# Two transformer blocks in one kernel: the down products on six PSUM banks, other queues, buffers and layout for the state space tables

## The chip, the cores and the metric

The kernel runs on one core of a Trainium2 chip. A core has TensorE (PE; its weight loads are listed apart as PEld), VectorE (DVE), ScalarE (ACT), GpSimd (POOL) and SyncE (SP), and 16 DMA engines that copy between the chip's memory and the on-chip memory. PE writes its results to PSUM, a small memory in banks, from which DVE and ACT read them; everything else lies in SBUF. SP and POOL each have a queue of their own from which they issue DMAs, and an instruction in a queue waits behind the one ahead of it.

The metric is the time of one execution on the device, in microseconds, as the median of several runs.

## The reference

One sequence of 1024 tokens with 1024 features goes through two blocks, in float32.

```python
x = layer_norm(ALPHA * x + 0.5 * swiglu(x, ffn1_w1, ffn1_w3, ffn1_w2), ln1_g, ln1_b)
q_lat, kv_lat, k_rope, u, g_a, g_b = split(x @ w_in)       # 384, 256, 32, 512, 1024, 1024 columns
y_a = mla_attention(q_lat, kv_lat, k_rope, ...) @ w_o_attn   # 8 heads; the latents are RMS-normed first
y_b = s5_branch(u, ...) @ w_o_ssm                            # 32 groups of 16 channels, 64 complex states
merged = sigmoid(g_a) * y_a + sigmoid(g_b) * y_b
x = layer_norm(ALPHA * x + merged @ w_out, ln2_g, ln2_b)
x = layer_norm(ALPHA * x + 0.5 * swiglu(x, ffn2_w1, ffn2_w3, ffn2_w2), ln3_g, ln3_b)
ple = sigmoid(x @ ple_w_gate) * (p @ ple_w_proj)
x = layer_norm(ALPHA * x + ple, ln4_g, ln4_b)
return second_block(x, ...)                                  # RG-LRU, convolutions, pooling, one gated mixer
```

`swiglu(x, w1, w3, w2) = (silu(x @ w1) * (x @ w3)) @ w2`, with 2816 hidden features. The S5 branch is a linear recurrence over the tokens in both directions. The kernel computes it in blocks of eight tokens, with tables made from the parameters: powers of the discretised state matrix times the input and output matrices B and C.

## The kernel before

Every matrix product is done in three passes: each float32 operand is split into a rounded high part and a remainder, and PE multiplies high by low, low by high and high by high. A split is a cast on ACT (L80) and a subtraction on DVE (L81). Weights pass through the ring `raw` (three buffers of 128 x 1024 words), loaded by SP; their parts are `wh` and `wl`.

PSUM has three rings: `up` (two tiles of two banks), `dn` (two tiles of one bank) and `tr` (two tiles of one bank). `tr` is for transposes above all, of the tables (L689, L709, L729, L730) as of the normalised rows (L144), and for the sums of squares (L955).

**The down projection** (`ffn_down`, called for both feed-forwards) computes the product of the hidden features `h` and the weights `V` by seven products of half size instead of eight. Product `i` has 11 steps of 12 matmuls (four row tiles `t`, three passes), 132 matmuls of 512 columns (L390). Products 0, 2, 4 and 6 write four half tiles of the two `up` tiles (`even`); products 1, 3 and 5 write two `dn` and two `tr` tiles (`odd`). After each product its four tiles are copied or added to `acc`, eight tiles of 128 x 1024 (ACT after products 0 and 1, DVE behind the others). Products 0 to 3 split the hidden features, which come back from memory, on the way; later ones load the parts. `half(0)`, after product 5, normalises the first four row tiles and transposes them into `x`, the input of the next projection; `half(1)` does so for the others after product 6. `affine` (L1269, L1270) then finishes the rows, and they are stored to `xd`.

**The tables** are made by a generator that hands over between two pieces of work. In the first feed-forward, `tick` runs it two steps at a time after each sixth of a product: `s5_setup`, then `s5_tables` for the batches 0 to 2 of eight, in the memory called `arena`. Per batch: POOL loads B and C (L684, L685), PE transposes C, DVE multiplies complex numbers in many small instructions (L470 to L477 and L654 to L658), PE transposes the results (L709, L729, L730), and POOL stores seven tables to `sd`. A second arena, opened after the first feed-forward in the memory that `acc` had, goes on with batches 3 to 7 beside the next projections; what it keeps of the first one comes by way of the memory `kd`.

**The gates** come after the latents: 16 blocks of 48 matmuls, each followed by a tanh into the ring `g` (two buffers) and a store to `gd` by SP (L933). Between them stand the five sums of squares of the latents (`squares`, L952 and L955, which use the same ring `g`) and, from the fifth block on, the state space batches: `s5_load` brings the tables (`s5b_tab`, L757, on SP) and the inputs (`s5b_U`, L760, eight loads on POOL), two batches ahead, and `s5_batch` begins with L782.

The order on each engine is made when the kernel is built, by a scheduler that simulates the engines with costs of its own. Program order decides which buffer of a ring a tile gets, and an instruction waits for whoever had that buffer before.

Of the kernel before, what the change touches and what calls it, by code (L numbers as in the profile page):

```python
# [8 lines left out]
F32 = mybir.dt.float32  # L9
# [8 lines left out]
P = 128  # L18
S = 1024
# [10 lines left out]
class Net:  # L30
# [314 lines left out]
    def ffn_down(self, fp, vr, acc, w2, hd, scale, load, half, tick=lambda: None):  # L345


        nc, v = self.nc, self.nc.vector
        hf, hs = hd
        NP = NF // 2  # L350
        units = [(i, min(2, NP - i)) for i in range(0, NP, 2)]
        wv = w2.rearrange("(q j p) m -> j p q m", j=2, p=P)
        rp = vr.enter_context(self.pool("vr", side="right"))

        first = [rp.tile([P, n, HALF], F32, name=self.uid("V")) for n in (8, NP - 8)]
        V = {k: rp.tile([P, NP, HALF], F32, name=self.uid("V")) for k in ((1, 1), (0, 1))}

        def at(k, ps):
            if k != (0, 0):
                return V[k][:, ps]  # L360
            return first[0][:, ps] if ps.stop <= 8 else first[1][:, ps.start - 8:ps.stop - 8]

        def loads(k):
            for p0, n in units:
                nc.sync.dma_start(at(k, slice(p0, p0 + n)), wv[k[0], :, p0:p0 + n, k[1] * HALF:(k[1] + 1) * HALF])

        def plus(x, y, op=ALU.add):
            v.tensor_tensor(out=x, in0=x, in1=y, op=op)

        def product(i, k, out, add=None, also=None):  # L370

            for u, (p0, n) in enumerate(units):
                ps = slice(p0, p0 + n)
                if add:
                    plus(at(k, ps), at(add, ps))
                if also:
                    also(ps)
                z = fp.tile([P, 2, 2, HALF], F32R, tag="v", bufs=2, name=self.uid("v"))
                self.split(at(k, ps), hi=z[:, 0, :n], lo=z[:, 1, :n])
                if i < 4:  # L380
                    h = self.split(self.raw(hf[i, :, ps], [P, n, HALF]))
                else:
                    h = [self.stream.tile([P, n, HALF], F32R, tag=tg, bufs=3, name=self.uid("h")) for tg in ("wh", "wl")]
                    for e in range(2):
                        nc.sync.dma_start(h[e].bitcast(F32), hs[i - 4, :, u, e, :n])
                for kk in range(n):
                    for t in range(4):
                        tk = slice(t * P, (t + 1) * P)
                        for m, (a, b) in enumerate(((0, 1), (1, 0), (0, 0))):
                            nc.tensor.matmul(out[t], lhsT=h[a][:, kk, tk], rhs=z[:, b, kk],  # L390
                                             start=u + kk + m == 0, stop=p0 + kk == NP - 1 and m == 2)
                tick()

        def even():
            ps = [self.up() for _ in range(2)]
            return [ps[j // 2][:, (j % 2) * HALF:(j % 2 + 1) * HALF] for j in range(4)]

        def odd():
            return [self.dn(), self.dn(), self.tr(), self.tr()]
        lo, hi = slice(0, HALF), slice(HALF, D)  # L400

        def residual(h):
            for t in range(h * 4, h * 4 + 4):
                x = self.stream.tile([P, D], F32, tag="raw", bufs=3, name=self.uid("res"))
                load(t, x)
                v.scalar_tensor_tensor(out=acc[t], in0=x, scalar=scale, in1=acc[t], op0=ALU.mult, op1=ALU.add)

        p = even()
        loads((0, 0))
        product(0, (0, 0), p)  # L410
        V[1, 0] = fp.tile([P, NP, HALF], F32, name=self.uid("V"))
        loads((0, 1))
        for t in range(4):
            nc.scalar.copy(acc[t][:, lo], p[t])
            nc.scalar.copy(acc[4 + t][:, lo], p[t])
        p = odd()
        product(1, (0, 0), p, add=(0, 1))
        loads((1, 0))
        for t in range(4):
            nc.scalar.copy(acc[t][:, hi], p[t])  # L420
            nc.scalar.copy(acc[4 + t][:, hi], p[t])
        p = even()
        product(2, (1, 0), p)
        loads((1, 1))
        for t in range(4):
            plus(acc[t][:, lo], p[t])
        p = odd()
        product(3, (1, 1), p)
        for t in range(4):
            plus(acc[t][:, hi], p[t])  # L430
        residual(0)
        p = even()
        product(4, (0, 0), p, add=(1, 1))
        for t in range(4):
            plus(acc[4 + t][:, lo], p[t])
            plus(acc[t][:, hi], acc[4 + t][:, lo], ALU.subtract)
        p = odd()
        product(5, (0, 1), p, add=(1, 1), also=lambda ps: plus(V[1, 0][:, ps], at((0, 0), ps)))
        for t in range(4):
            plus(acc[4 + t][:, lo], p[t])  # L440
            plus(acc[4 + t][:, hi], acc[4 + t][:, lo], ALU.subtract)
        vr.close()
        half(0)
        residual(1)
        p = even()
        product(6, (1, 0), p)
        for t in range(4):
            plus(acc[4 + t][:, lo], p[t])
        half(1)
# [6 lines left out]
GB = 4  # L456
# [3 lines left out]
class S5(Net):  # L460
# [96 lines left out]
    def s5_setup(self, arena):  # L557
# [14 lines left out]
        v.memset(at(2176, [P, G]), 0.0)  # L572
        nc.gpsimd.dma_start(dT, I["ssm_d"][0].rearrange("g c -> c g"))
        yield "pe"
        pt = self.tr()
        for i in range(2):
            nc.tensor.transpose(pt[:, i * G:(i + 1) * G], rows[:, i, :], self.ident[:G, :G])
# [83 lines left out]
    def s5_tables(self, arena, pool, sd, batches):  # L661
# [13 lines left out]
        vk = lambda z: z.rearrange("p (g a b) -> p g a b", g=GB, a=8)  # L675
        for i in range(2):
            v.memset(bd[i], 0.0)
        for b in batches:
            gs = slice(b * GB, (b + 1) * GB)
            R = [at(3840 + N * (i + 3 * (b % sets)), [P, N]) for i in range(3)]  # L680
            s4 = [pool.tile([P, N], F32, tag="tf", bufs=2, name=self.uid("s4")) for _ in range(2)]
            for d, s in enumerate("fb"):
                for i, nm in enumerate(("re", "im")):
                    nc.gpsimd.dma_start(B[d * 64:(d + 1) * 64, i], I[f"ssm_b_{nm}_{s}"][0, gs].rearrange("g p c -> p g c"))  # L684
                    nc.gpsimd.dma_start(crow[:, i, d * 64:(d + 1) * 64], I[f"ssm_c_{nm}_{s}"][0, gs].rearrange("g c p -> (g c) p"))  # L685
            yield "pe"
            pt = self.tr()
            for i in range(2):
# [3 lines left out]
            pair = lambda z: [z[:, 0], z[:, 1]]  # L692
            self.cmul(pair(bb), bc(be), pair(B), s2)
            self.cmul(pair(Br), bc(f), pair(bb), s2)
            yield

            def powers(tab, coef, o):
# [56 lines left out]

    def s5_load(self, b, pool, sd, ud):
        tab = pool.tile([P, 7, GB * NCH], F32, tag="s5b_tab", bufs=2, name=self.uid("s5b_tab"))
        self.nc.sync.dma_start(tab, sd[b])  # L757
        U = pool.tile([P, GB, NCH], F32, tag="s5b_U", bufs=2, name=self.uid("s5b_U"))
        for t in range(T8):
            self.nc.gpsimd.dma_start(U[t * C16:(t + 1) * C16],  # L760
                                   ud[b * GB * C16:(b + 1) * GB * C16, t, :].rearrange("(g c) k -> c g k", c=C16))
        return tab, U
# [67 lines left out]
class Mid(S5):  # L830
# [68 lines left out]
    def latents(self, xT, apool, gpool):  # L899
# [13 lines left out]
        for o, z in zip(wide, n0):  # L913
            z = z.bitcast(F32)
            nc.vector.tensor_copy(o[:, :, 0:96].rearrange("p k (a m) -> p k a m", a=3),
                                  z.unsqueeze(2).to_broadcast([P, KD, 3, 32]))
            nc.vector.tensor_copy(o[:, :, 96:112], z[:, :, 16:32])
            nc.vector.tensor_copy(o[:, :, 112:128], z[:, :, 0:16])
        p = self.up()
        for h in range(2):  # L920
            self.mm3(p[:, h * HALF:(h + 1) * HALF], [((wide[0][:, k], wide[1][:, k]), (xh(k, h), xl(k, h))) for k in range(KD)])
# [22 lines left out]
    def rms_latents(self, lat, tmp):  # L944
# [3 lines left out]
        sc = self.small.tile([P, 5, 8], F32, tag="rmss", bufs=1, name="rmss")  # L948

        def squares(k, tmp):  # L950
            t = tmp.tile([P, S], F32, tag="g", bufs=2, name=self.uid("sq"))
            nc.scalar.activation(out=t, in_=lat[k], func=AF.Square)  # L952
            ss = self.tr()
            for tt in range(8):
                nc.tensor.matmul(ss[:, tt:tt + 1], lhsT=t[:, tt * P:(tt + 1) * P], rhs=self.ones[:, 0:1], start=True, stop=True)  # L955
            v.tensor_copy(sc[:, k], ss[:, :8])
# [204 lines left out]
class Mix(Mid):  # L1161
# [133 lines left out]
    def block1(self):  # L1295
# [55 lines left out]
        xa.close()  # L1351
        q0.close()
        with self.pool("ffn1") as fp:
            acc = [fp.tile([P, D], F32, name=self.uid("acc")) for _ in range(8)]
            for nm in ("tf", "tf"):
                fp.tile([P, HALF], F32, tag=nm, bufs=2, name=self.uid("tf"))
            arena = fp.tile([P, 5376], F32, name="arena")
            kd = self.dram.tile([P, self.KEEP], F32, name="kd")

# [14 lines left out]
            def load(t, x):  # L1374
                nc.sync.dma_start(x, I["x"][0, t * P:(t + 1) * P, :])
# [20 lines left out]

        ap = LS.enter_context(self.pool("A"))
        self.rt = ap.tile([P, S], F32, name="rt")
        nc.sync.dma_start(self.rt[64:128], I["k_rope"])
        tabs = ExitStack()  # L1400
        tp = tabs.enter_context(self.pool("tabs"))
        arena = tp.tile([P, 6912], F32, name="arena")
# [863 lines left out]
```

## Time and profile before

| | us |
|---|---|
| median of 3 runs | 3318.21 (3316.32 to 3318.26) |
| profiled run | 3317.19 |
| its span in the profile | 3315.4 |
| PE busy | 3096.7 (93%) |
| DVE busy | 2455.5 (74%) |
| ACT busy | 1311.4 (40%) |
| POOL busy | 203.4 (6%) |

The shares are averages over stages with different limits. PE's mean granted clock over the span is 0.968 of full speed. A matmul that comes first after an idle stretch can run at the lower clock, so an idle stretch on PE costs more than its own length. In the page's strip of 40 slices PE has its lowest digits in slices 1, 6, 8, 9 and 10, and 12 and 13, that is in the first 80 us, from 480 to 520, from 600 to 840 and from 1000 to 1060 us.

### The profile page before, as it was taken

To read this page: it belongs to the slowest core of one execution; us is meant where nothing else is said; L and a number is where in the kernel's file an instruction comes from. 1 tells how busy PE (TensorE), PEld (TensorE's weight loads), DVE (VectorE), ACT (ScalarE), POOL (GpSimd) and SP (SyncE) were. 2 spreads that over 40 slices of the span, in tenths; PEclk is the share of its full clock that TensorE was granted. 3 is DMA by queue.
4 is the path that set the end of the run, shared out by engine and by line. 5 is a ranking of instruction groups with operands and counts; after the bars stand their busy time and mean duration, and the time that the engine had idled before them with its cause. 6 is when DMAs were issued, how large, how long until landed. Compare 5 with 4: busy or idle time off the path is not lost. (4 is left out here: it accounts for less than half of the span.)

```text
span 3315.4 us, 38710 instructions
## 1 busy us (share of the span) xinstructions
PE 3096.7 (93%) x14237; PEld 2516.1 (76%) x14237; DVE 2455.5 (74%) x4082; ACT 1311.4 (40%) x1857; POOL 203.4 (6%) x407
## 2 busy tenths in 40 slices
PE   6999988688996999999998999979989999999998
PEld 5788867566785878887876887868878788888786
DVE  6887767867565667776588886756778498898668
ACT  4233323223221136663263333333244456555443
POOL 0000000211343320000000000000000000000000
PEclk8999999898997999999998999989999999999999
DMA  3543445354534520004454544363733222322545
GB/s 121 160 151 121 134 162 182 107 201 137 161 111 142 172 82 9 17 7 159 165 169 137 165 146 124 130 250 105 245 116 109 89 70 82 97 85 72 193 159 182
DMA packets 334011, 433.17 MB, mean 131 GB/s; under 512 B 29861, under 2 KB 218302, under 8 KB 332542
## 3 DMA queue, kind: packets, MB, share of 16 engines
q1 hardware_dynamic: 319486, 408.45, 37.6%
q0 software_dynamic: 14336, 22.26, 2.2%
q8 instruction: 112, 1.84, 0.2%
q14 instruction: 77, 0.63, 0.1%
HBM read 311.00 MB, written 119.62 MB: 130 GB/s over the span
## 5 line engine op out<-in xcount | busy, mean ns | idle before, releaser
L101 PE MATMUL up<-x,wh 128*128 128x512 f32 x2336 | 755.8, 400 | 15.2 <-DVE x L81 13.9
L101 PEld LDWEIGHTS up<-x,wh 128*128 128x128 f32 x2336 | 442.5, 190 | 125.8 <-DVE x L81 16.9
L80 ACT CAST wh<-raw 128x1024 fp32r<-128x1024 f32 (+2 forms) x305 | 307.6, 1011 | 426.9 <-PE up L176 179.3
L101 PE MATMUL up<-x,wl 128*128 128x512 f32 x1168 | 465.5, 399 | 0.3 <-DVE wl L81 0.3
L81 DVE TENSOR_TENSOR wl<-raw,wh 128x1024 fp32r<-128x1024 f32 (+2 forms) x305 | 356.6, 1170 | 144.1 <-ACT wh L80 143.4
L1260 PE MATMUL up<-wh,x 128*128 128x512 f32 x1024 | 319.4, 393 | 0.0
L101 PEld LDWEIGHTS up<-x,wl 128*128 128x128 f32 x1168 | 221.9, 190 | 52.4 <-DVE wl L81 0.8
L1260 PEld LDWEIGHTS up<-wh,x 128*128 128x128 f32 x1024 | 192.2, 188 | 41.9 <-DVE x L81 0.8
L1260 PE MATMUL up<-wl,x 128*128 128x512 f32 x512 | 201.9, 396 | 2.5 <-ACT xf L2157 1.8
L80 ACT CAST v<-V 128x1024 fp32r<-128x1024 f32 x84 | 82.2, 981 | 271.4 <-PE up L390 127.5
L81 DVE TENSOR_TENSOR v<-V,v 128x1024 fp32r<-128x1024 f32 x84 | 94.9, 1131 | 93.2 <-ACT v L80 93.1
L390 PE MATMUL up<-v,wh 128*128 128x512 f32 x352 | 117.5, 412 | 41.1 <-DVE v L81 41.0
L80 ACT CAST wh<-S 128x1024 fp32r<-128x1024 f32 x88 | 73.3, 833 | 204.4 <-PE dn L176 141.8
L2078 DVE SCALAR_TENSOR_TENSOR cv<-u,kc,cv 128x1024 f32<-128x1024 f32 x120 | 153.0, 1275 | 1.2
L390 PE MATMUL up<-v,h 128*128 128x512 f32 x528 | 126.1, 394 | 0.7 <-DVE v L81 0.7
L1260 PEld LDWEIGHTS up<-wl,x 128*128 128x128 f32 x512 | 96.1, 188 | 26.3 <-ACT xf L2157 2.4
L390 PEld LDWEIGHTS up<-v,wh 128*128 128x128 f32 x352 | 70.3, 200 | 59.1 <-DVE v L81 43.7
L390 PEld LDWEIGHTS up<-v,h 128*128 128x128 f32 x528 | 97.5, 188 | 22.6 <-DVE v L81 2.7
L176 PE MATMUL up<-x4l,wh 128*128 128x512 f32 x176 | 73.3, 416 | 42.9 <-ACT wh L80 41.4
L101 PE MATMUL up<-k,qh 128*128 128x512 f32 x256 | 93.1, 406 | 2.3 <-ACT e L1087 2.3
L80 ACT CAST ph<-tr 128x512 fp32r<-128x512 f32 x128 | 73.6, 587 | 51.7 <-PE tr L1100 50.7
L81 DVE TENSOR_TENSOR pl<-tr,ph 128x512 fp32r<-128x512 f32 x128 | 85.6, 682 | 10.6 <-ACT ph L80 10.1
(651 smaller groups left out, 7058.8 us busy)
## 6 DMA issues: line engine op xcount, KB each, us to landing
raw<-in_ffn_w_dram SPq DMA_DIRECT2D x96, 512.0 KB
raw<-in_w_in_dram SPq DMA_DIRECT2D x69, 512.0 KB
hs<-sp SPq DMA_DIRECT2D x66, 512.0 KB
h<-hs SPq DMA_DIRECT2D x60, 512.0 KB
raw<-in_w_out_dram SPq DMA_DIRECT2D x52, 512.0 KB
raw<-hf SPq DMA_DIRECT2D x40, 512.0 KB
V<-in_ffn_w_dram SPq DMA_DIRECT2D x40, 512.0 KB
s5b_tab<-sd SPq DMA_DIRECT2D x8, 1792.0 KB
```

The costliest lines, as they stand in the source:

```text
L80: (copy or nc.scalar.copy)(hi, x)
L81: nc.vector.tensor_tensor(out=lo, in0=x, in1=hi.bitcast(F32), op=ALU.subtract)
L101: nc.tensor.matmul(out, lhsT=a, rhs=b, start=i == 0, stop=i == n - 1)
L176: nc.tensor.matmul(out, lhsT=w[a][:, k], rhs=x[b][:, kx], start=start and i == 0, stop=stop and i == 11)
L390: nc.tensor.matmul(out[t], lhsT=h[a][:, kk, tk], rhs=z[:, b, kk], start=u + kk + m == 0, stop=p0 + kk == NP - 1 and m == 2)
L1260: self.nc.tensor.matmul(o, lhsT=a, rhs=b[:, c], start=k == 0 and m == 0, stop=k == K - 1 and m == 2)
L2078: v.scalar_tensor_tensor(out=st["y"], in0=u[:, j:j + S], scalar=k, in1=st["y"], op0=ALU.mult, op1=ALU.add)
```

## The change

There are five edits.

1. `odd` takes two `dn` tiles and one `up` tile (its two halves for row tiles 2 and 3) instead of two `dn` and two `tr`. The list `late` empties the `up` halves first. Where a result goes to two places in `acc`, the second is now made from the first in SBUF, in a loop of its own.
2. `s5_setup` yields once more before its first transpose. `s5_tables` loads B and C for the next batch right after their last use in this one.
3. `s5_load` issues the load of the tables from POOL instead of SP.
4. In the pool of the first feed-forward the two `tf` tiles come first, then `acc` in reverse, so that other tiles lie where the second arena is opened. The load of `rt` (the rope table) is issued later, among the latents.
5. `squares` takes its buffer from the ring `raw` instead of `g`.

```diff
         def odd():
-            return [self.dn(), self.dn(), self.tr(), self.tr()]
+            ps = [self.dn(), self.dn(), self.up()]
+            return ps[:2] + [ps[2][:, :HALF], ps[2][:, HALF:]]
+        late = (2, 3, 0, 1)
...
         for t in range(4):
             nc.scalar.copy(acc[t][:, lo], p[t])
-            nc.scalar.copy(acc[4 + t][:, lo], p[t])
+        for t in range(4):
+            nc.scalar.copy(acc[4 + t][:, lo], acc[t][:, lo])
...
         p = odd()
         product(3, (1, 1), p)
-        for t in range(4):
+        for t in late:
             plus(acc[t][:, hi], p[t])
...
+        yield "pe"
         yield "pe"
         pt = self.tr()
...
+        def load(b):
+            gs = slice(b * GB, (b + 1) * GB)
+            for d, s in enumerate("fb"):
+                for i, nm in enumerate(("re", "im")):
+                    nc.gpsimd.dma_start(B[d * 64:(d + 1) * 64, i], I[f"ssm_b_{nm}_{s}"][0, gs].rearrange("g p c -> p g c"))
+                    nc.gpsimd.dma_start(crow[:, i, d * 64:(d + 1) * 64], I[f"ssm_c_{nm}_{s}"][0, gs].rearrange("g c p -> (g c) p"))
+        load(batches[0])
         for b in batches:
...
             self.cmul(pair(Br), bc(f), pair(bb), s2)
+            if b != batches[-1]:
+                load(b + 1)
             yield
...
-        self.nc.sync.dma_start(tab, sd[b])
+        self.nc.gpsimd.dma_start(tab, sd[b])
...
+        nc.sync.dma_start(self.rt[64:128], self.I["k_rope"])
         p = self.up()
...
-            t = tmp.tile([P, S], F32, tag="g", bufs=2, name=self.uid("sq"))
+            t = self.stream.tile([P, S], F32, tag="raw", bufs=3, name=self.uid("sq"))
...
-            acc = [fp.tile([P, D], F32, name=self.uid("acc")) for _ in range(8)]
             for nm in ("tf", "tf"):
                 fp.tile([P, HALF], F32, tag=nm, bufs=2, name=self.uid("tf"))
+            acc = [fp.tile([P, D], F32, name=self.uid("acc")) for _ in range(8)][::-1]
...
-        nc.sync.dma_start(self.rt[64:128], I["k_rope"])
```

The edits also move instructions on the engines, since the scheduler orders anew. Line numbers after the change are 13 to 14 higher from `s5_tables` on: the table transposes L689, L709, L729 and L730 are L700, L722, L742 and L743 there, the squares' matmuls L955 are L969, and L782 is L795. Three places matter.

On PE, in product 3 of the first down projection (its tiles are `dn_4618`, `dn_4619`, `tr_4620`, `tr_4621`), before:

```order
2300 L390 MATMUL dn_4619<-v_4658,wl_4664 128x512
2301 L390 MATMUL dn_4619<-v_4658,wh_4663 128x512
2302 L689 MATMUL tr_4235<-ident,arena 128x64 x2
2303 L709 MATMUL tr_4313<-ident,arena 128x128 x4
2304 L709 MATMUL tr_4320<-ident,arena 128x128 x4
2305 L729 MATMUL tr_4455<-arena 64x128
2306 L689 MATMUL tr_4589<-ident,arena 128x64 x2
2307 L390 MATMUL tr_4620<-v_4622,wh_4627 128x512
2308 L390 MATMUL tr_4620<-v_4622,wl_4628 128x512
```

and the same product now (its tiles are `dn_4598`, `dn_4599` and `up_4600`):

```order
2272 L390 MATMUL dn_4599<-v_4601,wh_4606 128x512
2273 L390 MATMUL dn_4599<-v_4601,wl_4607 128x512
2274 L390 MATMUL dn_4599<-v_4601,wh_4606 128x512
2275 L390 MATMUL up_4600<-v_4601,wh_4606 128x512
2276 L390 MATMUL up_4600<-v_4601,wl_4607 128x512
```

Before, two units of the product on the `dn` tiles are followed by the transposes of two table batches, and the `tr` tiles come after them. Now the four tiles of a step follow each other, and the first table transpose (L700) stands at row 2392, at the end of the product.

On DVE, at the same product, before (`arena` holds the tables; the split ahead of these rows, of `v_4658`, is row 781, and the next one, of `v_4705`, row 902):

```order
786 L470 TENSOR_TENSOR arena<-arena 128x256
787 L471 TENSOR_TENSOR arena<-arena 128x256
788 L472 TENSOR_TENSOR arena<-arena 128x256
789 L470 TENSOR_TENSOR arena<-arena 128x32
790 L471 TENSOR_TENSOR arena<-arena 128x32
791 L472 TENSOR_TENSOR arena<-arena 128x32
792 L475 TENSOR_TENSOR arena<-arena 128x256
```

and now, where L470 to L477 are L476 to L483, and `V` and `raw` are what is split:

```order
797 L481 TENSOR_TENSOR arena<-arena 128x256
798 L81 TENSOR_TENSOR v_4744<-V_3615,v_4744 128x1024
799 L481 TENSOR_TENSOR arena<-arena 128x32
800 L482 TENSOR_TENSOR arena<-arena 128x256
801 L661 TENSOR_TENSOR arena<-arena 128x512
802 L81 TENSOR_TENSOR wl_4789<-raw_4786,wh_4788 128x1024
803 L482 TENSOR_TENSOR arena<-arena 128x32
```

The rows before are part of 120 table instructions in a row. Now a split stands after 31 of them at most, here after two to four.

On PE, in the gate stage, where the last tables are transposed and the first state space batch begins, before:

```order
3629 L729 MATMUL tr_7100<-arena 64x128
3630 L730 MATMUL tr_7100<-arena 64x128
3631 L955 MATMUL tr_7212<-ones,sq_7210 128x1 x8
3632 L955 MATMUL tr_7282<-ones,sq_7280 128x1 x8
3633 L782 MATMUL up_7305<-s5b_U_7143,s5b_tab_7141 128x128 x8
3634 L816 MATMUL dn_7344<-s5b_U_7143,s5b_tab_7141 128x128
3635 L101 MATMUL up_7373<-x_5380,wh_7369 128x512
```

and now:

```order
3588 L101 MATMUL up_7225<-x_5378,wl_7222 128x512
3589 L101 MATMUL up_7225<-x_5378,wh_7221 128x512
3590 L969 MATMUL tr_7279<-ones,sq_7277 128x1 x8
3591 L743 MATMUL tr_7097<-arena 64x128
3592 L742 MATMUL tr_7097<-arena 64x128
```

The sums of squares stood between the last transpose and the first batch; the second of them now stands in row 3590, the first in row 3585, ahead of the last transposes; the first batch (L795) follows these directly, in row 3598. On POOL the table load of a batch stands directly ahead of its eight U loads for batches 0 and 1, and behind them for the others.

## Rows read from the trace of the kernel before

**Rows 1.** The page, busy time, share of the span and instructions of each engine.

```profile
PE 3096.7 (93%) x14237; PEld 2516.1 (76%) x14237; DVE 2455.5 (74%) x4082; ACT 1311.4 (40%) x1857; POOL 203.4 (6%) x407
```

**Rows 2.** Windows: length, busy us of PE, PEld, DVE, ACT, POOL; clock, DMA share, GB/s.

```profile
600.60:784.60 184.00, 146.09 (x638) 116.07 (x638) 133.39 (x292) 46.69 (x59) 44.46 (x84) 0.89 0.50 169
700.00:740.00 40.00, 29.61 (x110) 23.06 (x109) 23.01 (x58) 10.42 (x11) 3.28 (x7) 0.83 0.40 145
784.60:836.00 51.40, 35.33 (x128) 26.14 (x129) 37.10 (x70) 14.93 (x20) 0.00 (x0) 0.78 0.27 96
860.00:1000.00 140.00, 140.00 (x668) 111.47 (x667) 82.58 (x173) 33.73 (x46) 56.53 (x107) 1.00 0.38 115
1000.00:1046.00 46.00, 18.16 (x84) 15.85 (x83) 11.22 (x30) 7.92 (x10) 18.61 (x37) 0.66 0.51 170
1020.00:1040.00 20.00, 3.03 (x15) 2.94 (x14) 0.39 (x5) 1.46 (x2) 11.53 (x23) 0.50 0.80 272
1046.00:1190.00 144.00, 143.83 (x756) 121.81 (x756) 101.63 (x173) 25.45 (x31) 48.54 (x96) 0.99 0.52 155
2220.00:2420.00 200.00, 199.25 (x893) 163.20 (x891) 144.02 (x181) 74.94 (x92) 0.00 (x0) 1.00 0.52 173
```

**Rows 3.** Timeline of PE, 597 to 647: start, us, instruction, count, [idle before, releaser].

```profile
597.81 0.39 PE L390 MATMUL up<-v,wl 128*128 128x512 f32 x1
...
600.08 0.39 PE L390 MATMUL up<-v,wh 128*128 128x512 f32 x1
...
620.48 0.46 PE L689 MATMUL tr<-ident,arena 64*128 64x64 f32 x2 [11.84 <-DMA arena<-in_ssm_c_re_f_dram]
...
646.66 0.80 PE L390 MATMUL dn<-v,wh 128*128 128x512 f32 x1 [3.87 <-DVE v L81]
```

**Rows 4.** Timeline of DVE, two splits of V that follow each other.

```profile
604.32 1.22 DVE L81 TENSOR_TENSOR v<-V,v 128x1024 fp32r<-128x1024 f32 x1
...
645.40 1.21 DVE L81 TENSOR_TENSOR v<-V,v 128x1024 fp32r<-128x1024 f32 x1
```

**Rows 5.** Waits of PE, 660 to 780: us in total, times, longest.

```profile
PE dn L390 <- DVE v L81: 7.0, 2, 5.3
PE tr L709 <- DVE nq L109: 2.3, 1, 2.3
PE tr L709 <- DVE nq L113: 1.1, 1, 1.1
```

**Rows 6.** The first window of rows 2, matmuls of L390 alone (PE, PEld).

```profile
600.60:784.60 184.00, 132.13 (x528) 102.87 (x528) 0.89 0.50 169
```

**Rows 7.** Groups of DVE, 600.6 to 784.6: count, busy us, mean ns, idle before.

```profile
L368 DVE TENSOR_TENSOR acc<-acc,up 128x512 f32<-128x512 f32 x8 | 5.0, 678 | 0.0
L81 DVE TENSOR_TENSOR x<-tf,x 128x512 fp32r<-128x512 f32 x7 | 4.6, 686 | 2.2 <-ACT x L80 2.2
L150 DVE TENSOR_SCALAR tf<-tr,vecs 128x512 f32<-128x512 f32 x4 | 3.2, 802 | 0.4 <-PE tr L144 0.4
```

**Rows 8.** Timeline of PE in the gate stage.

```profile
1041.13 3.57 PE L955 MATMUL tr<-ones,sq 128*128 128x1 f32 x16 [18.10 <-ACT sq L952]
1044.57 3.76 PE L782 MATMUL up<-s5b_U,s5b_tab 128*128 128x128 f32 x16
```

**Rows 9.** Timelines of SP's queue and of ACT, same stage.

```profile
1024.64 0.81 SPq L757 DMA_DIRECT2D s5b_tab<-sd  x2
...
1040.02 1.06 ACT L952 ACTIVATE sq<-lat 128x1024 f32<-128x1024 f32 x1 [15.87 <-DMA gd<-g]
```

**Rows 10.** DMA issues, 1000 to 1300: count, KB each, median us to landing.

```profile
s5b_tab<-sd SPq DMA_DIRECT2D x8, 1792.0 KB
...
s5b_U<-ud POOLq DMA_DIRECT2D x64, 32.0 KB, 7.2
```

**Rows 11.** Timeline of POOL, the U loads of two batches.

```profile
1064.22 4.04 POOL L760 DMA_DIRECT2D s5b_U<-ud  x8 [26.14 <-PE dn L817]
...
1109.53 4.04 POOL L760 DMA_DIRECT2D s5b_U<-ud  x8 [17.58 <-PE dn L817]
```

More of the change, by code (lines that the diff above doesn't have):

```diff
@@ L418, in ffn_down @@
         loads((1, 0))
-        for t in range(4):
+        for t in late:
             nc.scalar.copy(acc[t][:, hi], p[t])
-            nc.scalar.copy(acc[4 + t][:, hi], p[t])
+        for t in late:
+            nc.scalar.copy(acc[4 + t][:, hi], acc[t][:, hi])
         p = even()
@@ L428, in ffn_down @@
         product(3, (1, 1), p)
-        for t in range(4):
+        for t in late:
             plus(acc[t][:, hi], p[t])
@@ L435, in ffn_down @@
             plus(acc[4 + t][:, lo], p[t])
+        for t in range(4):
             plus(acc[t][:, hi], acc[4 + t][:, lo], ALU.subtract)
@@ L438, in ffn_down @@
         product(5, (0, 1), p, add=(1, 1), also=lambda ps: plus(V[1, 0][:, ps], at((0, 0), ps)))
-        for t in range(4):
+        for t in late:
             plus(acc[4 + t][:, lo], p[t])
+        for t in late:
             plus(acc[4 + t][:, hi], acc[4 + t][:, lo], ALU.subtract)
@@ L681, in s5_tables @@
             s4 = [pool.tile([P, N], F32, tag="tf", bufs=2, name=self.uid("s4")) for _ in range(2)]
[L682 to L685, printed above, removed]
             yield "pe"
```

## The prediction

> **What bounds the kernel now.** I read the page first, then PE by stretches of time, then its timeline and waits where it is idle. The page [rows 1] shows PE busy for 3096.7 us of a span of 3315.4: an edit is worth what it takes out of the 219 us of idle, and of the stretches beside them at the lower clock. The profiled run took 3317.19 us, so 1.8 us lie around the span; the median of the three runs shown, 3318.21, is 1.0 us above that run. I sum against the profiled run and add the 1.0 at the end.
>
> The stretches [rows 2] show where the idle time stands in the part that the change touches. Products 3 to 6 of the first down projection (600.6 to 784.6 us) last 184.0 us with PE busy 146.1 and a mean granted clock of 0.89. The tail behind them (to 836) lasts 51.4 with PE busy 35.3. In the gate stage, 1000 to 1046, PE works 18.2 of 46. The down projection of the second feed-forward, which has no tables beside it, is busy 199.25 of 200 us: the product loop as such has nothing to give.
>
> Inside products 3 to 6 the first stall is the large one. PE's timeline [rows 3] shows it standing 11.84 us for a table transpose (L689) at 620.48, which waits for the load of its operand; it comes back to the `dn` columns of product 3 only at 646.66. Product 3's last two columns could not be written meanwhile, because both `tr` banks belonged to the tables. DVE meanwhile ran tables: between the split of V at 604.32 and the next at 645.40 there is none [rows 4]. Later in the same products PE waits 7.0 + 2.3 + 1.1 us for DVE, while DVE normalises half 0 [rows 5].
>
> **Part 1: six PSUM banks, table loads a batch ahead, the extra stop in the setup.** These have one answer. Product 3 now writes `dn`, `dn` and one `up` tile, so no table transpose stands in front of its columns: the first moves from PE row 2302 to row 2392, the end of product 3. The B and C loads are issued right after the previous batch's last use of their buffers, so L689's 11.84 us go, unless DVE is late. On DVE the block of 120 table instructions between two splits of V becomes at most 31.
>
> What bounds the stretch then? PE's floor: ten matmul starts lie between 597.81 and 600.08 [rows 3], 0.227 us each; 4 products x 132 x 0.227 = 119.9 us. All other PE work in the stretch is 146.1 - 132.1 = 14.0 us [rows 2, 6], together 134. DVE's floor: 133.4 us busy [rows 2], less the seven L81 x splits and four L150 of half 0 (4.6 + 3.2 = 7.8 us) [rows 7], which now stand behind product 6: 125.6. The two are close, so I don't take the floor of PE. The 10.4 us of waits on half 0's norm [rows 5] have not lost their cause; I keep them, and 3.4 us for the lower clock beside them (a granted 0.83 over the 40 us from 700 leaves 6.8 us short, and half of that is PE's own). 134 + 14 = 148 us against 184: **-36**. The bounds are 134 (PE never waits: -50) and 168 (the tables keep half of what they took: -16). I take 148, nearer to 134, because the row without tables shows the loop itself running without a break.
>
> **The tail.** Half 0's 32 feature transposes (L144) stood inside product 6; they now come after it, since the two `tr` banks they rotate through are held by table tiles that trail. So 7.8 us of DVE work move from beside product 6 to the tail, on top of 37.1 us there [rows 2]: 44.9 at least, 51.4 + 7.8 = 59.2 at most. PE has only 24 of the next matmuls to put between them. I take 55.4, near the upper end, because the x splits stand in one queue with sixteen affine operations there: **+4** (-6.5 to +7.8).
>
> **The new bank ring.** An odd product's `up` tile takes the slot of the even product before it. Its first `up` column comes after six `dn` matmuls, 1.4 us; emptying two half tiles is two additions of 0.68 us [rows 7], queued behind at most one split of 1.2 [rows 4]. So a change of product costs 0 to 2 us, and there are six in each projection; the second one is fully busy now, so nothing there hides a wait. I take **+1** in each, bounds 0 and +6. The evacuation copies that now read SBUF stay on ACT, which is busy 47 of the 184 us: nothing, and about 0.5 us per change if ACT were late.
>
> **Part 2: the squares and the table load (gates).** PE stands 18.10 us before the squares' matmuls L955 at 1041.13 [rows 8]: ACT's square waited 15.87 us for the `gd<-g` store to free the ring, and that store stood on SP behind the two L757 loads, which left at 1024.64 when the table stores had landed [rows 9]. With the square in the weight ring both squares' matmuls stand before L730 and wait for no store. Next is L782, and now its operands are late: from 1024.64 POOL issues the table (1792 KB, 6.6 us at the 272 GB/s of 1020 to 1040 in rows 2) and then eight U loads (4.0 us of issue, 7.2 to land) [rows 10, 11]. U is the last: 1024.6 + 0.5 + 4.0 + 7.2 = 1036.3. L782 started at 1044.57, so **-8**; the 7 us of square matmuls move into the idle time and are in the 8. Were U there as soon as it is issued, it would be -15; with both tables ahead of it on the wires (13.2 us) and U behind, -1. A new wait comes along: a weight load needs a ring slot that PE must first read at L955, and the rest of SP's queue stands behind it. The next gate's 48 matmuls (11 us) cover one load; uncovered it would be 512 KB at the 170 GB/s of 1000 to 1046, 3 us for each of five squares.
>
> **Part 3: layout and the rope load.** The second arena now lies under columns that finish earlier. But PE is busy without a break from 860 to 1000 with DVE at 83 of 140 us [rows 2], so an earlier start is hidden: 0, down to -4 if the last table ended earlier too. The rope load waits for nothing where it now stands: 0.
>
> Sum: -36 + 4 + 1 + 1 - 8 = -38; 3317.2 - 38 + 1.0 = **3280 us**.
>
> **A rule against the table load's move.** The eight U loads of a batch leave POOL in 4.04 us [rows 11], 0.505 each, in a stretch where DVE is busy 101.6 of 144 us [rows 2]. The Trainium skill (SBUF — State Buffer, "Who interferes with whom") says that a DMA issued by GpSimd can be held up by DVE, because GpSimd writes the descriptors through a port pair that it shares with DVE, and that issuing it from a hardware queue ends this. The trace's even 0.505 us does not show it; by the rule the load had better stayed on SP, and the third rival is what it would do here.
>
> **Rivals.**
> 1. The stall only moves. DVE's floor is 125.6 of 148 us, and half 0 now ends later: the stretch takes 168 us (-16), the tail 59 (+8), the ring +2, the gates -4. That is -10: 3308. For it: all of PE's later waits [rows 5] are for DVE, and DVE and PE have nearly the same floor. Against: no block of more than 31 table instructions is left.
> 2. Both stalls go with their low clock: 134 us (-50), tail 45 (-6), gates -15, arena -4, ring 0: -75, 3243. Against: the waits of [rows 5] keep their cause.
> 3. Slower: POOL's queue becomes the bound of the eight state space batches. In a pair of batches (1064.22 to 1109.53) POOL idles 17.6 us [rows 11]. Two table loads in that queue bring 2 x (0.5 + 6.6) = 14.2 if something behind waits for their landing, so 3.4 are left. Were POOL's 32 issues of 0.5 us in a pair also twice as long beside DVE, +16, each pair would be 13 over; three pairs cost 39 us and the gates' gain is gone: -36 + 4 + 2 + 39 = +9, 3327. The kernel gets slower from 10 us over per pair. Against: the loads are issued two batches ahead.
> 4. It doesn't do what it says: tables still come between, since they trail and now hold `tr` ahead of half 0's features; the stretch gains 6, the tail gives it back, the gates gain 1: 3317.
>
> **Chances.** The forecast 0.62, with a range of its own from 3262 to 3299 (the stretch -50 to -18, tail and gates within their bounds, not all at one end). Rival 1 0.15; rival 2 0.08; rival 3 0.07; rival 4 0.08. For 8 times in 10 the range runs from 3252, half way to rival 2, to 3311, which takes in rival 1. About 0.2%, 6.6 us, can be told from no change. Faster is the forecast with rivals 1 and 2: 0.85; same is rival 4: 0.08; slower is rival 3: 0.07.
>
> **What would show it.** Right: no gap of 11.84 us in product 3; PE idle under 18 us from product 3 to the end of product 6, which ends 30 us or more earlier; in the gates no wait for the square, and in its place one of 10 to 15 us before L782, on a DMA. Wrong: PE's waits for the V splits in products 3 to 6 as long in sum as before (rival 1); PE waiting for U or the table in each batch after 1046 (rival 3); in the second projection waits of `up` for the additions at every change of product, above 2 us each.

## The result, and the profile after

The changed kernel takes **3258.01 us** (median of four runs, 3256.48 to 3260.63), against 3318.24 of the kernel before in the same measurement; the ratio is 0.982, 95% interval 0.9808 to 0.9832. That is 60 us less where 38 were forecast. The direction held, and so did the range for 8 times in 10, 3252 to 3311; the forecast's own, 3262 to 3299, was missed by 4 us. The profiled run took 3256.48 us, with a span of 3254.7.

The page's first line shows the same work with less idle time on PE, 174 us of the span instead of 219 [rows 1]:

```profile
PE 3080.6 (95%) x14237; PEld 2507.4 (77%) x14237; DVE 2457.0 (75%) x4082; ACT 1312.7 (40%) x1857; POOL 207.9 (6%) x415
```

The windows that answer to rows 2 are products 3 to 6, the tail behind them, and the gate stage up to the first state space batch (length, busy us of PE, PEld, DVE, ACT and POOL, then clock, DMA share, GB/s):

```profile
598.00:732.50 134.50, 129.68 (x592) 104.59 (x590) 121.61 (x283) 39.21 (x47) 35.25 (x66) 1.00 0.66 220
732.50:784.00 51.50, 34.24 (x147) 25.72 (x147) 43.31 (x85) 21.53 (x32) 14.46 (x27) 0.75 0.32 112
955.00:995.00 40.00, 14.94 (x84) 12.62 (x83) 12.28 (x37) 5.81 (x8) 17.32 (x34) 0.64 0.58 178
980.00:995.00 15.00, 0.16 (x1) 0.19 (x2) 0.00 (x0) 0.00 (x0) 7.56 (x16) 0.50 0.63 194
```

Products 3 to 6 last 134.5 us instead of 184.0, at a granted clock of 1.00. DVE did not bound them: it is busy 121.6 us. All waits of PE in them are these three groups (us in total, times, longest), 4.8 us where rows 3 and 5 show single waits as long as 11.84:

```profile
PE up L390 <- DVE v L81: 2.8, 2, 2.4
PE dn L390 <- DVE v L81: 1.6, 1, 1.6
PE up L390 <- DVE acc L368: 0.4, 1, 0.4
```

On DVE the splits of V, of which two lay 41 us apart [rows 4], now follow each other every 3 to 11 us in the stretch; the first four:

```profile
601.61 1.22 DVE L81 TENSOR_TENSOR v<-V,v 128x1024 fp32r<-128x1024 f32 x1
605.03 1.22 DVE L81 TENSOR_TENSOR v<-V,v 128x1024 fp32r<-128x1024 f32 x1
610.06 1.23 DVE L81 TENSOR_TENSOR v<-V,v 128x1024 fp32r<-128x1024 f32 x1
615.50 1.22 DVE L81 TENSOR_TENSOR v<-V,v 128x1024 fp32r<-128x1024 f32 x1 [0.27 <-ACT v L80]
```

In the gate stage PE no longer waits for the square (L969 is L955 of before, L795 is L782). It waits in one piece, for the inputs of the first batch [rows 8]:

```profile
961.87 1.95 PE L969 MATMUL tr<-ones,sq 128*128 128x1 f32 x16
...
994.84 3.75 PE L795 MATMUL up<-s5b_U,s5b_tab 128*128 128x128 f32 x16 [23.03 <-DMA s5b_U<-ud]
```

POOL's timeline shows what it waits for. The table's load waits 3.17 us for the table stores; four U loads follow, three more after 2.68 us, and the eighth only when the table has landed, at 992.65:

```profile
977.04 4.06 POOL L755 DMA_DIRECT2D sd<-arena  x8
984.27 0.57 POOL L770 DMA_DIRECT2D s5b_tab<-sd  x1 [3.17 <-DMA sd<-arena]
984.90 2.02 POOL L773 DMA_DIRECT2D s5b_U<-ud  x4
989.60 1.52 POOL L773 DMA_DIRECT2D s5b_U<-ud  x3 [2.68 <-issue]
992.65 0.51 POOL L773 DMA_DIRECT2D s5b_U<-ud  x1 [1.54 <-DMA s5b_tab<-sd]
```

How far the changed kernel is ahead at points of the program tells where the 60.7 us of the span came from. The points are starts of a line's matmuls in the two profiles, first, last or counted:

| point | before | after | ahead |
|---|---|---|---|
| last matmul of product 2 | 600.1 | 597.7 | 2.4 |
| last matmul of product 6 | 783.8 | 732.1 | 51.7 |
| matmul 145 of the next projection (L101) | 849.5 | 804.4 | 45.1 |
| matmul 501 of the next projection (L101) | 941.9 | 896.8 | 45.1 |
| last table transpose (L730) | 1013.7 | 971.4 | 42.3 |
| first state space batch (L782) | 1044.6 | 994.8 | 49.8 |
| first attention transpose (L1100) | 1238.8 | 1185.8 | 53.0 |
| last of the second up projection (L176) | 2180.3 | 2121.6 | 58.7 |
| first of the second down projection (L390) | 2191.4 | 2131.3 | 60.1 |
| last of the second down projection (L390) | 2419.8 | 2361.3 | 58.5 |
| last row transpose (L144) | 2597.5 | 2536.3 | 61.2 |
| end of the span | 3315.4 | 3254.7 | 60.7 |

### The profile page after: what moved, and what is told of

It reads as the page before. It is cut to its first block, busy times and chain, and to the rows that moved or that the text cites. A ratio compares the mean times of both kernels' runs of the same rounds, so it can differ in the third digit from the quotient of the medians.

```text
span 3254.7 us, 38683 instructions
## 1 busy us (share of the span) xinstructions
PE 3080.6 (95%) x14237; PEld 2507.4 (77%) x14237; DVE 2457.0 (75%) x4082; ACT 1312.7 (40%) x1857; POOL 207.9 (6%) x415
## 4 chain that ended last, share of the span: by engine, by line
PE 47%; DVE 4%; DMA 3%; ACT 1%; issue 0%; SPq 0%; DVEq 0%; ACTq 0%
PE up L101 17%; PE up L1274 10%; PE up L176 6%; PE dn L176 5%; PE up L390 4%; PE dn L101 3%; PE dn L390 1%; DMA V<-in_ffn_w_dram 1%; DVE wl L81 0%; DMA gb<-gd 0%; PE tr L144 0%; DMA raw<-in_mod_w_dram 0%; DMA y<-yd 0%; DMA hs<-sp 0%; DVE x L81 0%
## 5 line engine op out<-in xcount | busy, mean ns | idle before, releaser
L101 PE MATMUL up<-x,wh 128*128 128x512 f32 x2336 | 756.1, 400 | 7.9 <-DVE x L81 7.1
L101 PEld LDWEIGHTS up<-x,wh 128*128 128x128 f32 x2336 | 442.4, 190 | 116.7 <-DVE x L81 9.5
L101 PE MATMUL up<-x,wl 128*128 128x512 f32 x1168 | 465.9, 399 | 4.8 <-DVE wl L81 4.8
L101 PEld LDWEIGHTS up<-x,wl 128*128 128x128 f32 x1168 | 221.9, 190 | 57.0 <-DVE wl L81 5.7
L390 PE MATMUL up<-v,wh 128*128 128x512 f32 x528 | 177.8, 405 | 39.8 <-DVE v L81 39.8
L390 PE MATMUL up<-v,h 128*128 128x512 f32 x660 | 159.0, 393 | 4.9 <-DVE v L81 4.5
L390 PEld LDWEIGHTS up<-v,wh 128*128 128x128 f32 x528 | 103.7, 196 | 64.1 <-DVE v L81 41.5
L390 PEld LDWEIGHTS up<-v,h 128*128 128x128 f32 x660 | 122.3, 188 | 33.2 <-DVE v L81 7.3
L176 PE MATMUL up<-x4l,wh 128*128 128x512 f32 x176 | 72.6, 412 | 38.7 <-ACT wh L80 36.0
L390 PE MATMUL up<-v,wl 128*128 128x512 f32 x264 | 106.5, 403 | 0.0
L101 PE MATMUL up<-k,qh 128*128 128x512 f32 x256 | 93.0, 406 | 2.3 <-ACT e L1101 2.3
L80 ACT CAST ph<-tr 128x512 fp32r<-128x512 f32 x128 | 73.5, 587 | 51.7 <-PE tr L1114 50.5
```

Of the source, the lines that this page charges most:

```text
L80: (copy or nc.scalar.copy)(hi, x)
L101: nc.tensor.matmul(out, lhsT=a, rhs=b, start=i == 0, stop=i == n - 1)
L176: nc.tensor.matmul(out, lhsT=w[a][:, k], rhs=x[b][:, kx], start=start and i == 0, stop=stop and i == 11)
```

## The experiments

All times are medians of four runs; the kernel before, measured beside them, is a median of seven.

| run | us | before | ratio, 95% interval |
|---|---|---|---|
| tr_banks | 3294.09 | 3315.80 | 0.9933 (0.9918 to 0.9948) |
| banks_only | 3268.71 | 3315.80 | 0.9853 (0.9837 to 0.9870) |
| tab_on_sp | 3262.69 | 3315.80 | 0.9839 (0.9825 to 0.9854) |
| squares_in_g | 3263.42 | 3315.80 | 0.9840 (0.9825 to 0.9854) |
| loads_late | 3259.75 | 3316.25 | 0.9827 (0.9813 to 0.9842) |
| layout_before | 3258.56 | 3316.25 | 0.9824 (0.9810 to 0.9839) |
| batches_later | 3270.21 | 3316.25 | 0.9857 (0.9841 to 0.9874) |
| batches_two_later | 3265.55 | 3316.25 | 0.9850 (0.9835 to 0.9864) |
| gates_both_undone | 3270.73 | 3316.83 | 0.9862 (0.9847 to 0.9877) |
| four_batches_later | 3251.35 | 3316.83 | 0.9805 (0.9790 to 0.9820) |
| four_later_u_first | 3253.67 | 3316.83 | 0.9805 (0.9789 to 0.9822) |

The intervals are 9 to 11 us wide, so differences of 3 to 5 us between kernels are read from places in the profiles and not from these times.

**The banks taken away: tr_banks.** In the changed kernel:

```diff
-            ps = [self.dn(), self.dn(), self.up()]
-            return ps[:2] + [ps[2][:, :HALF], ps[2][:, HALF:]]
-        late = (2, 3, 0, 1)
+            return [self.dn(), self.dn(), self.tr(), self.tr()]
+        late = (0, 1, 2, 3)
```

> The changed kernel, with the odd products on two dn and two tr banks again (and emptied in the old order); all else as changed. Theory: the banks are what removes the stall in products 3 to 6, since a table transpose no longer holds a bank that the product needs. Then the stretch from product 3 to the end of product 6 takes 165 us or more again instead of 132, and the kernel 3285 to 3305 us. Rival: the table loads a batch ahead removed it, because the largest wait was on a load; then the stretch stays under 140 us and the kernel takes 3256 to 3265.

Measured 3294.09: 38 of the 60 us are lost again. The stall is back, though B and C are loaded a batch ahead in this kernel. Its PE timeline shows it (L699 is L689 of before),

```profile
621.37 0.46 PE L699 MATMUL tr<-ident,arena 64*128 64x64 f32 x2 [13.61 <-DMA arena<-in_ssm_c_re_f_dram]
```

and its POOL timeline shows why the load ahead can't help there: the loads of the first batches, issued from 611.39 on, wait for DVE, which has not done with the setup.

```profile
611.39 0.54 POOL L690 DMA_DIRECT2D arena<-in_ssm_c_im_f_dram  x1 [14.48 <-DVE arena L482]
```

The stretch lasts 176.2 us (599.9 to 776.1). The load was late because DVE was; PE stood because the tables held the product's banks.

**The banks alone: banks_only.** In the kernel before, `odd`, `late` and the order of the evacuation of the change:

```diff
         def odd():
-            return [self.dn(), self.dn(), self.tr(), self.tr()]
+            ps = [self.dn(), self.dn(), self.up()]
+            return ps[:2] + [ps[2][:, :HALF], ps[2][:, HALF:]]
+        late = (2, 3, 0, 1)
...
```

> The kernel before, with the odd products on two dn tiles and one up tile and nothing else. Theory of the banks: most of the stretch's gain is there alone, 132 to 145 us from product 3 to the end of product 6, and the kernel takes 3265 to 3280 us (the gate stage as before, which the change did not shorten by more than 3 us). Rival, the loads: the wait for the table load stays and with it half of the stall; 3290 us or more.

Measured 3268.71, 47 us less than before. All but 2 us of the stretch's gain is there without the other edits; products 3 to 6 in its profile, and PE's waits in them:

```profile
597.90:734.10 136.20, 131.23 (x591) 105.78 (x590) 121.43 (x283) 39.20 (x47) 35.23 (x66) 0.99 0.65 218
PE up L390 <- DVE v L81: 2.8, 2, 2.4
PE dn L390 <- DVE v L81: 1.7, 1, 1.7
PE up L390 <- DVE acc L368: 0.4, 1, 0.4
```

At the last table transpose this kernel is 42.8 us ahead of before (the changed kernel 42.3), and at the first batch still 42.6: the gate stage gave it nothing.

**The other half of part 1: loads_late.** In the changed kernel, B and C loaded at the start of their own batch:

```diff
-        load(batches[0])
         for b in batches:
+            load(b)
...
-            if b != batches[-1]:
-                load(b + 1)
```

> The changed kernel, with B and C loaded at the start of their own batch again. In the run with the old banks the wait of 13.61 us for this load came back although the load was a batch ahead. Theory: the load of a batch is early enough in either place once the product doesn't wait for the tables; stretch 131 to 135 us, kernel 3255 to 3262. Rival: table transposes wait for the loads (about 2 us to land, three batches) and PE behind them: 3263 to 3270.

Measured 3259.75, and at the last table transpose 43.4 us ahead. The load ahead is worth nothing that can be measured here.

**Layout: layout_before.** In the changed kernel, `acc` ahead of the `tf` tiles in program order, and the rope load at its old place:

```diff
+            acc = [fp.tile([P, D], F32, name=self.uid("acc")) for _ in range(8)]
             for nm in ("tf", "tf"):
                 fp.tile([P, HALF], F32, tag=nm, bufs=2, name=self.uid("tf"))
-            acc = [fp.tile([P, D], F32, name=self.uid("acc")) for _ in range(8)][::-1]
...
```

> The changed kernel, with the layout and the place of the rope load as before. Theory: the second arena then waits for the last rows of acc again, 30 us longer, but PE has no idle time between the tail and the last tables that this could make longer: 3255 to 3262. Rival: the tables of the second arena end later by what they begin later, since DVE and POOL carry them; the start of the first batch then moves by 5 us or more: 3263 to 3275.

Measured 3258.56; the last table transpose is 40.2 us ahead, the first batch 47.1. The second arena opens 32 us later (795.66, in the changed kernel 763.46), and little hangs on that: the layout is worth nothing to the total, and 2 to 3 us at this place, as much as single profiles scatter.

**The gates: tab_on_sp, squares_in_g, gates_both_undone.** In the changed kernel the first edit, the second, and both:

```diff
-        self.nc.gpsimd.dma_start(tab, sd[b])
+        self.nc.sync.dma_start(tab, sd[b])
...
-            t = self.stream.tile([P, S], F32, tag="raw", bufs=3, name=self.uid("sq"))
+            t = tmp.tile([P, S], F32, tag="g", bufs=2, name=self.uid("sq"))
```

> The changed kernel, with the table load of the state space batches on SP again. Theory: in the changed kernel PE waits 23.03 us before the first batch because the eighth U load stands on POOL behind the table's landing (issued at 992.65, 8.4 us after the table). On SP the eight U loads leave directly behind the table stores, and PE waits for the table alone: the wait falls to 15 to 20 us, the kernel takes 3251 to 3257. Rival: the two tables share the wires again and the first lands as late as the last U load did; wait 22 to 26 us, 3256 to 3261.

> The changed kernel, with the squares in the ring g again. Theory: the squares were no bound any more, since the tables and U land last; the squares' matmuls come in the time in which PE waits anyway, and the first batch starts within 3 us of the changed kernel's: 3256 to 3261. Rival: the wait for the gate store comes back at full length, behind the start of the first batch, and costs 8 us or more: 3266 to 3275.

> The changed kernel, with the table load on SP and the squares in the ring g, both as before. Each of the two undone alone kept the gate stage's gain (the first batch 7 to 9 us earlier, counted from the last table transpose). Theory: the chain of before needs both, a square that waits for a gate store and a store that stands behind the table loads; with both undone the wait before the squares' matmuls is 18 us again and the first batch starts 30 to 31 us after the last table transpose instead of 23: 3263 to 3270. Rival: the gain comes from the layout or from the earlier tables; the wait stays near 23 us: 3257 to 3262.

Measured 3262.69, 3263.42 and 3270.73. The waits of PE from 960 to 1010, with the table on SP:

```profile
PE up L795 <- DMA s5b_U<-ud: 23.7, 1, 23.7
```

with the squares in `g`:

```profile
PE tr L969 <- ACT sq L966: 7.4, 2, 5.3
PE up L795 <- DMA s5b_U<-ud: 7.0, 1, 7.0
```

and with both undone, where the wait before the squares is that of rows 8:

```profile
PE tr L969 <- ACT sq L966: 23.6, 2, 18.3
PE tr L743 <- ACT arena L731: 4.4, 1, 4.4
```

From the last table transpose to the first batch it takes 30.9 us before, 31.0 with both undone, 23.4 in the changed kernel, 24.1 with the table on SP and 21.9 with the squares in `g`. So the gain of 7 to 9 us needs one of the two edits and not both: either the square doesn't need the store, or the store doesn't stand behind the table. The theory for tab_on_sp was wrong by its number. The eighth U load does leave earlier, at 988.07 instead of 992.65, but both tables are then in flight (issued from 983.41 on). It takes 8.3 us from issue to landing instead of 2.0, and the first batch starts no sooner: the rival's outcome. In tab_on_sp, the tables' issue and the time to landing of its first eight U loads:

```profile
983.41 0.82 SPq L770 DMA_DIRECT2D s5b_tab<-sd  x2
DMA to landing us min/median/max: 2.0/6.8/8.3
```

In squares_in_g the gate stage is as fast as the theory had it; its total lies 2 us above the forecast, and a later gain is missing in it (the second up projection, below).

There is a second, smaller effect of the table's queue, which I had not looked for. From the first batch to the first attention transpose the kernels with the table on POOL gain 3.0 to 3.6 us on before (changed kernel, tr_banks, squares_in_g, loads_late, layout_before), those with the table on SP -0.4 to 0.1 (tab_on_sp, banks_only, gates_both_undone). The wait that differs is that of ACT for the cast of an attention weight, with the table on SP:

```profile
ACT wq L80 <- DMA zd<-s5b_z: 5.4, 1, 5.4
```

and in the changed kernel:

```profile
ACT wq L80 <- DVE v L81: 2.9, 1, 2.9
```

**What is left in the gates: batches_later, batches_two_later.** PE waits 23 us for the first batch with no gate block left in front of it. In the changed kernel the batches come one block later, and in the second run two:

```diff
-            if i >= 4 and i % 3:
+            if i >= 5 and (i - 1) % 3:
```

> The changed kernel, with every state space batch one gate block later. Theory: what is left of the gate stage is a wait of 23.03 us for the inputs of the first batch with nothing else in PE's order; 48 more matmuls in front of it (11 us at full clock) run in that time: wait about 12 us, kernel 3244 to 3249. Rival: the time comes back behind the gates, where the last batch has no gate beside it (its DVE work is about 17 us a batch): 3253 to 3262.

> The changed kernel, with every state space batch two gate blocks later, the last one behind the gates. Theory: 96 matmuls (22 us) cover the whole wait of 23 us, and the low clock behind it: 3233 to 3242 if the end of the stage loses nothing. Rival: the last batch stands alone behind the gates, PE waits for DVE there for 10 us or more: 3245 to 3258.

Measured 3270.21 and 3265.55, both slower than the changed kernel. The wait did shrink, to 5.0 us for U and 5.7 for the block put in front; but the last batch then stands at the end of the gates, and PE waits there for DVE (first run, 1140 to 1200):

```profile
PE dn L830 <- DVE s5b_w L825: 12.9, 1, 12.9
PE dn L101 <- DVE v L81: 4.5, 1, 4.5
```

The rival held in kind: time won at one end of a chain of batches was lost at the other. Both times lie about 8 us above its ranges, so the loss was larger than it said.

**Only the first batches later: four_batches_later, four_later_u_first.** Only the first batches move; the last ones stay where they were. The second run also has U ahead of the table in each load.

```diff
-            if i >= 4 and i % 3:
+            if i in (5, 6, 7, 8, 10, 11, 13, 14):
```

> The changed kernel, with the batches after the gate blocks 5, 6, 7, 8, 10, 11, 13, 14 instead of 4, 5, 7, 8, 10, 11, 13, 14. Theory: moving all batches gave the wait at their start (23 to 5 us) but lost it at the end, where the last batch stood too late (a wait of 12.88 us for DVE). Here only the first two move and the end stays: the start gains 10 us, 3244 to 3251. Rival: DVE needs about 17 us a batch and three in a row are then too close, so a wait for DVE comes at the third or fourth batch: 3254 to 3262.

> The kernel with the batches after the gate blocks 5, 6, 7, 8, 10, 11, 13, 14, and in each load of a batch the eight U loads ahead of the table on POOL. Theory: the last U load stood behind the landing of the table (issued 8.4 us after it); ahead of it, U is there 5 us or more earlier and only the table (issued about 984) is waited for; what is left of the first wait falls by 2 to 5 us more: 3240 to 3249. Rival: the table then leaves after U and lands later by as much: no difference to the kernel without this edit, within 2 us.

Measured 3251.35 and 3253.67. The first is 0.9805 of before, 6.7 us under the changed kernel by medians. The intervals overlap, so the times alone leave it open; the profile supports it: at the last L795 of the batches (L782 of before) this kernel is 57.0 us ahead of before, the changed kernel 49.1. Its waits from 960 to 1010:

```profile
PE up L101 <- ACT g L946: 5.5, 1, 5.5
PE up L795 <- DMA s5b_U<-ud: 4.7, 1, 4.7
PE tr L743 <- ACT arena L731: 2.0, 1, 2.0
```

U first brought nothing: from the last table transpose to the first batch it takes 29.4 us, in its twin 24.9. POOL's timeline shows the U loads waiting for the table stores, and the table, 10 us later than in its twin, behind them. U reads nothing that these stores write, so the wait is probably for the memory that they still read; no run shows that.

```profile
988.98 2.53 POOL L771 DMA_DIRECT2D s5b_U<-ud  x5 [4.76 <-DMA sd<-arena]
994.13 1.52 POOL L771 DMA_DIRECT2D s5b_U<-ud  x3 [2.62 <-issue]
995.64 0.57 POOL L774 DMA_DIRECT2D s5b_tab<-sd  x1
```

## Why the prediction was right, and where it was off

**Products 3 to 6, forecast -36, measured -49.5** (184.0 to 134.5). The mechanism was right and is shown by taking the banks away and by adding them alone. The term that was mis-sized is the one that I kept: 10.4 us of waits on half 0's norm and 3.4 for the clock beside them, which "have not lost their cause". They had: with the banks alone all waits of PE in the stretch sum to 4.9 us. I had read them as waits for DVE. But in the longest, 5.32 us, DVE itself stood, for ACT's cast of V, and that cast stood behind the four activations of the norm (L134). Before:

```profile
719.88 4.64 ACT L134 ACTIVATE acc<-acc,nq 128x1024 f32<-128x1024 f32 x4 [0.86 <-DVE nq L132]
724.43 1.98 ACT L80 CAST v<-V 128x1024 fp32r<-128x1024 f32 x2
725.49 2.36 DVE L81 TENSOR_TENSOR v<-V,v 128x1024 fp32r<-128x1024 f32 x2 [5.51 <-ACT v L80]
726.77 2.50 PE L390 MATMUL dn<-v,h 128*128 128x512 f32 x5 [5.32 <-DVE v L81]
```

After, the norm's activations take as long, but a cast stands ahead of them, and PE doesn't wait there:

```profile
681.87 1.05 ACT L80 CAST v<-V 128x1024 fp32r<-128x1024 f32 x1 [6.34 <-PE up L390]
682.83 4.64 ACT L134 ACTIVATE acc<-acc,nq 128x1024 f32<-128x1024 f32 x4
```

banks_only has the same order (681.82 and 682.77). So the norm's work is still there; what went is an order in which it stopped PE. The 3.4 us of waits at L709 were table transposes that stood in the product's order.

The stretch is as long as the lower bound that I worked out, 134, which was rival 2's stretch, but that is in part luck: not 119.9 of product and 14.0 of other work, but 123.9 and 5.8, and 4.8 of waits. Half 0's transposes, which I had counted in the 14.0, moved into the tail. The two floors being close had kept me from PE's, but DVE's busy time, 121.6, leaves it 13 us of air.

Part 1 was costed with one answer for three edits. The banks carry it; the load ahead was given credit for L689's 11.84 us and has none: the wait is back in tr_banks, with the load ahead, and stays away in loads_late without it. The extra stop in the setup is not in banks_only, which has nearly the whole gain without it.

**The tail, forecast +4, measured +6.6** (51.7 us ahead at the last matmul of product 6, 45.1 from matmul 145 of the next projection on), within its bounds. banks_only loses 6.0 between the same points and tr_banks nothing (8.1 and 8.9 ahead), so the loss comes with the banks, as forecast.

**The ring of banks, forecast +1 and +1.** In the first projection the waits for an addition sum to 0.4 us; the second loses 1.6 us from its start to its end (60.1 to 58.5 ahead).

**The gates, forecast -8, measured -7.5** from the last table transpose on. Just ahead of that point 2.8 us are lost (45.1 to 42.3 ahead), where the squares' matmuls, 3.8 us in all, now stand in front of the last transposes; counted from matmul 501 the gates give -4.7. U's landing set the end as forecast: the first batch starts 13.7 us after POOL issued the last table store (981.1 to 994.84), where the estimate came to 12.9. That the sum came so close is luck: the eight U loads took 8.3 us to issue and not 4.0, and the last one landed 2.0 us after its issue and not 7.2. The wait before the first batch is 23.03 us, longer than the 10 to 15 that I gave as a sign. The ground I gave was too narrow: not the square's ring, but either of the two edits.

**Layout, forecast 0:** 0 within what can be told, in layout_before.

**Not in the sum: 11 us more** behind the gates, and 2.4 ahead of product 3, where the runs scatter from 0.2 to 3.1. Without the 11 us the time would lie in the forecast's own range. 3.2 are the queue of the table load, at the start of attention, as shown above. 5.7 come in the second up projection, where before PE waits 7.37 us at 2007.50, and after 2.08 for the same:

```profile
2007.50 0.80 PE L176 MATMUL up<-x4l,wh 128*128 128x512 f32 x1 [7.37 <-ACT wh L80]
```

Ten of the eleven runs have this gain (4.2 to 6.6 between the same two points), tr_banks and banks_only among them. squares_in_g has not: PE waits 7.65 us there at 1955.41. gates_both_undone has the squares in `g` too and has the gain, so it belongs to no single edit; no run isolates it, and it stays open. The 2.7 us in the rows behind the second down projection are there in all runs with the banks (1.0 to 2.7) and not in tr_banks (-0.7), so they seem to come with the banks.

Of the rivals, the second had the stretch right, but its tail (-6) and its gates (-15) did not come. The third, POOL as the bound of the batches, did not come either: the changed kernel is 49.8 us ahead at the first batch and 49.1 at the last, and POOL still idles in a pair of batches, though each table took 8.2 us to land (median) and not 7.1. The eight U loads keep the pace of rows 11:

```profile
1014.62 4.03 POOL L773 DMA_DIRECT2D s5b_U<-ud  x8 [11.67 <-PE dn L829]
...
1060.38 4.03 POOL L773 DMA_DIRECT2D s5b_U<-ud  x8 [15.16 <-PE dn L830]
```

The rule of the Trainium skill (SBUF — State Buffer, "Who interferes with whom") that spoke against the move of the load shows no effect here: 0.50 us per U load beside a busy DVE, and the load's old queue was no faster (a wait of 23.7 us before the first batch in tab_on_sp, 23.0 in the changed kernel). That does not test the rule: the section names copies, casts and tensor_scalar as the operations that can take the shared ports from GpSimd, and reports no stalled DMA beside tensor_tensor. Beside the U loads at 1014.62 and 1060.38 DVE ran only tensor_tensor and one scan each time. I had left that condition out.

## What to carry to other kernels

Work beside a stream of matmuls should have PSUM banks of its own: a bank that both rotate through makes the stream wait in PE's order for whatever the side work waits for. A wait is not kept because the work behind it is still there: follow it to the instruction that stood in the way, and ask whether it still stands there in the new order. Where a wait has two conditions, test the edits apart: here either alone was enough. A move at the start of a chain of batches was only a gain when the end of the chain stayed where it was.

## What I had not expected of the hardware

On POOL's queue of this kernel a DMA waits for the landing of the one issued eight before it. In the changed kernel's trace none of the 377 DMAs of this queue leaves earlier, and their landings are told by eight semaphores (counters that instructions wait for), used in turn. The eighth U load stood until the table, 1792 KB, had landed: it left at 992.65, 8.4 us after the table, though it doesn't need it. Whether the chip asks for this or the way the program is built, no run shows. Behind the later tables the eighth small store stands 3.2 to 4.6 us in the same way. I had counted the issue of eight U loads as 4.0 us; there it took 8.3.
